# A decoder layer's feed-forward block: Strassen's seven products for gate and up, and the down projection in a second phase

## The chip, the cores and the metric

The kernel runs on one core of a Trainium2 chip. The metric is the device time of one execution in microseconds (us); the kernel before was timed in three runs.

## The reference

One layer of a hybrid decoder, for 1024 prompt tokens (one sequence) and 64 sample tokens (8 sequences of 8). All is float32, the model width D is 1024 and the feed-forward width FF is 2816. The change is in the last part, `back`:

```python
def back(x, f, u_out, o, p):
    nsa = o.reshape(B, T, Q_W) @ p['w_nsa_o']
    mix = (f['g_conv'] * u_out + f['g_nsa'] * nsa) @ p['w_out']
    x = x + f['g1'] * mix
    h = rms_norm(x, p['ffn_norm_g']) * (1.0 + f['sc2']) + f['sh2']
    ffn = (jax.nn.silu(h @ p['w_gate']) * (h @ p['w_up'])) @ p['w_down']
    return x + f['g2'] * ffn
```

Before it the layer computes the modulation vectors, one input projection, a convolution branch and an attention branch. None of that is touched.

## The kernel before, in words

**Numbers in two pieces.** A float32 operand is split into `hi` (the value in the type `F32R`, copied by ACT) and `lo` (the rest, one subtraction on DVE or POOL). A product of 128 rows is three matmuls on TensorE (PE), hi·hi, hi·lo and lo·hi, made by `mm3` (lines 338 to 340). For the sample tokens the two pieces lie side by side in 128 columns and two matmuls do (`mm2`, lines 343 and 344). Line 152 is the copy `acopy`, line 158 is `sub_sb`, the subtraction that alternates between DVE and POOL.

**Order.** The program is written in tiles from pools with a number of buffers; a scheduler that simulates the program settles the order of each engine's queue, and the engines wait for each other by semaphores. Each engine works its queue in order.

**The stages at issue** begin near 1030 us. The *m loop* (line 1482 on) multiplies the attention output by `w_nsa_o`, merges it with the convolution branch and splits the result into `mh_` and `ml_`, in three chunks of 384, 384 and 320 tokens; in between, `w_out` is loaded and split. *The out projection* is `out_half(i, j)`: nine token tiles, two column halves, 24 matmuls of 512 columns each. Its results are scaled by the gate and added to x in the tiles `x1`, which stay in SBUF to the end. `norm2` normalizes finished tiles, transposes them on PE (line 1573), applies the modulation on DVE (line 1576, `hf`) and splits the result into the same tiles `mh_`, `ml_`, now called `h2h`, `h2l`.

**The feed-forward block.** FF is worked in NF = 22 tiles of 128. `up_tile(t)` multiplies the three chunks by the gate and the up weights (8 blocks of 128 rows each): 2 x 8 x 3 x 3 = 144 matmuls, of which 96 have 384 columns and 48 have 320. Sigmoid and two multiplications follow (lines 1659 to 1661), then the split of the activations (line 1664). After every second t, `down` multiplies the two activation tiles by `w_down`, and adds the scaled sum into `x1` (lines 1697 and 1698), eleven times 18 pieces: nine token tiles by two halves. So gate/up and down alternate in one long run of matmuls, and the activations never leave SBUF:

```python
        for t in range(NF):
            up_tile(t)
            if t % 2 == 0 and t:
                down([t - 2, t - 1], False)
        down([NF - 2, NF - 1], True)
```

## Time and profile before

| | |
|---|---|
| time, median of 3 runs | 2002.25 us (1992.97 to 2007.45) |
| profiled execution, own time | 1995.01 us |
| its span, first to last instruction | 1993.2 us |
| mean granted TensorE clock | 0.981 |
| PE / DVE / ACT / POOL busy | 1903.5 / 1332.6 / 714.7 / 742.0 us |
| first matmul of gate/up, last matmul of all | 1200.06 us, ends 1985.69 us |

The views of the trace are the page with its busy times, windows (busy time of each engine in a stretch), groups of equal instructions, and the timeline of single instructions. Matmuls overlap in the pipeline: a row's length is longer than the step from one start to the next, and it is the step that a stream of them costs.

### The profile page before, as it was taken

The numbers are of one execution on the slowest core, as the hardware profiler recorded it, in microseconds if no ns is written. First come the engines' busy times: TensorE is split into PE (matmuls) and PEld (weight loads), VectorE is DVE, ScalarE is ACT, GpSimd is POOL, SyncE is SP. The second block draws the span as 40 slices with busy tenths as digits, with TensorE's granted clock in tenths as the row PEclk, the third lists the DMA queues.
The fourth block names the chain that finished last, engine by engine and source line by source line (L and its number), as shares of the span: only waits on it lengthen the run. The fifth ranks groups of instructions, "written<-read, shape, count | busy, mean of one in ns | idle before, by whom it ended". The sixth has DMA issues, their size and how long they took to land.

```text
span 1993.2 us, 29739 instructions
## 1 busy us (share of the span) xinstructions
PE 1903.5 (95%) x11036; PEld 1710.5 (86%) x11036; DVE 1332.6 (67%) x2217; ACT 714.7 (36%) x1711; POOL 742.0 (37%) x737
## 2 busy tenths in 40 slices
...
GB/s 298 180 231 219 113 110 156 104 176 110 146 176 128 177 129 126 48 14 7 1 79 223 112 1 79 61 43 43 43 54 42 43 53 33 43 53 38 48 11 90
DMA packets 170823, 191.37 MB, mean 96 GB/s; under 512 B 13847, under 2 KB 135719, under 8 KB 170606
## 3 DMA queue, kind: packets, MB, share of 16 engines
...
## 4 chain that ended last, share of the span: by engine, by line
PE 54%; DVE 2%; DMA 1%; issue 1%; POOL 1%; ACT 0%; SPq 0%; DVEq 0%; POOLq 0%; ACTq 0%
PE pf L338 10%; PE pf L339 10%; PE pf L340 10%; PE pt L340 4%; PE pt L339 4%; PE pt L338 4%; PE pT L1396 3%; PE po L1403 2%; PE po L1404 2%; PE pS L1355 1%; PE pS L1357 1%; DMA w<-in_w_out 1%; PE pS L1360 1%; DVE x L1698 0%; PE pt L343 0%
## 5 line engine op out<-in xcount | busy, mean ns | idle before, releaser
L338 PE MATMUL pf<-mh,wh 128*128 128x384 f32 (+1 forms) x1032 | 336.7, 326 | 0.0
L340 PE MATMUL pf<-mh,wl 128*128 128x384 f32 (+1 forms) x1032 | 336.5, 326 | 0.0
L339 PE MATMUL pf<-ml,wh 128*128 128x384 f32 (+1 forms) x1032 | 336.5, 326 | 0.0
L1664 POOL TENSOR_TENSOR actl<-sg,acth 128x384 fp32r<-128x384 f32 (+1 forms) x66 | 66.4, 1006 | 488.5 <-ACT acth L152 488.5
L338 PE MATMUL pd<-hh,whi 128*128 128x384 f32 (+1 forms) x576 | 194.8, 338 | 11.0 <-DVE U L1058 8.2
L338 PEld LDWEIGHTS pf<-mh,wh 128*128 128x128 f32 x1032 | 193.7, 188 | 7.3 <-DVE sg L1661 3.0
L340 PEld LDWEIGHTS pf<-mh,wl 128*128 128x128 f32 x1032 | 193.7, 188 | 4.0
L339 PEld LDWEIGHTS pf<-ml,wh 128*128 128x128 f32 x1032 | 193.7, 188 | 3.1
L339 PE MATMUL pd<-hl,whi 128*128 128x384 f32 (+1 forms) x576 | 193.2, 335 | 0.0
L340 PE MATMUL pd<-hh,wlo 128*128 128x384 f32 (+1 forms) x576 | 191.8, 335 | 1.1 <-DVE wlo L270 1.1
L1092 DVE SCALAR_TENSOR_TENSOR y<-U,wdT,y 128x1024 f32<-128x1024 f32 x120 | 162.0, 1350 | 0.6
L1698 DVE TENSOR_TENSOR x<-x,dt 128x512 f32<-128x512 f32 x180 | 146.4, 813 | 5.4
L340 PE MATMUL pt<-wdh,actl 128*128 128x512 f32 x352 | 139.0, 395 | 0.0
L339 PE MATMUL pt<-wdl,acth 128*128 128x512 f32 x352 | 138.5, 393 | 0.0
L338 PE MATMUL pt<-wdh,acth 128*128 128x512 f32 x352 | 137.1, 389 | 0.0
L1659 ACT ACTIVATE sg<-pf 128x384 f32<-128x384 f32 (+1 forms) x66 | 30.8, 467 | 295.7 <-PE pf L340 295.7
L1660 DVE TENSOR_TENSOR sg<-sg,pf 128x384 f32<-128x384 f32 (+1 forms) x66 | 34.9, 529 | 146.0 <-ACT sg L1659 146.0
L1697 DVE TENSOR_TENSOR dt<-pt,indgp 128x512 f32<-128x512 f32 x160 | 110.7, 692 | 26.3 <-PE pt L340 11.3
L338 PEld LDWEIGHTS pd<-hh,whi 128*128 128x128 f32 x576 | 110.6, 192 | 19.3 <-DVE U L1058 8.6
L1384 POOL TENSOR_SCALAR P<-P,ast 128x640 f32<-128x640 f32 (+7 forms) x128 | 89.2, 723 | 70.1 <-DVE ast L1380 68.2
L338 PE MATMUL pz<-whi,hh 128*128 128x256 f32 (+1 forms) x320 | 97.5, 306 | 18.4 <-ACT zt L152 11.3
L152 ACT ACTIVATE whi<-wraw 128x512 fp32r<-128x512 f32 (+1 forms) x133 | 81.1, 624 | 92.1 <-PE pd L339 49.5
...
## 6 DMA issues: line engine op xcount, KB each, us to landing
...
```

The lines of the kernel that those rows point to most:

```text
L152: S.activation(out, in_, AF.Copy, scale=scale)
L338: PE.matmul(out, ah, bh, start=first, stop=False)
L339: PE.matmul(out, ah, bl, start=False, stop=False)
L340: PE.matmul(out, al, bh, start=False, stop=last)
L1092: V.scalar_tensor_tensor(op, U[:, k:k + TP], wk, op, op0=ALU.mult, op1=ALU.add)
L1384: G.tensor_scalar(P_[br][g][:, :w], P_[br][g][:, :w], st[:, 2, br, g:g + 1], 1.0, op0=ALU.mult, op1=ALU.mult)
L1396: PE.transpose(pT[:nk, g * 128:(g + 1) * 128], a, ident)
L1403: PE.matmul(po, va, ph[:nk], start=(bi == 0), stop=False)
L1404: PE.matmul(po, va, pl_[:nk], start=False, stop=(bi == len(blocks) - 1))
L1664: G.tensor_tensor(al[:, c0:c0 + n], sg_[:, :n], f(ah[:, c0:c0 + n]), op=ALU.subtract)
L1697: V.tensor_tensor(tmp, p, gx[:, cs_], op=ALU.mult)
L1698: (G if last and j == 0 else V).tensor_tensor(x1[i][:, cs_], x1[i][:, cs_], tmp, op=ALU.add)
```

## The change

Everything up to the m loop stays. Then:

- The tokens are put in two columns u: u = 0 the first 512 prompt tokens, u = 1 the other 512 and the 64 sample tokens. Each u has two halves r of 256 or 288 columns (`SEG`). The split values are in quarter tiles `qh`, `ql` by row half a and segment; `ms` holds the sample's pieces for the out projection.
- `w_out` comes in blocks of 128 rows by 512 columns. The out projection does all nine tiles of j = 0 first, then those of j = 1, with `norm2` after every two tiles. `x1` is written to memory (`x1_d`) and read again at the end.
- Gate and up are the two row blocks of one matrix, and this matrix, of 2 x 2 blocks, times the 2 x 2 blocks of h is made by seven products in place of eight. `build(u)` makes the four combined right-hand blocks of h and splits them (in tiles `tq`), once; `load_up(t)` makes four combined left-hand blocks of the weights and splits all seven (tiles `aw`, one set of 14); the products' sums are made on DVE out of PSUM. Each product is 4 x 3 = 12 matmuls, of 256 columns for u = 0 and 288 for u = 1.
- The gated activations go to memory (`act_d`), not to split tiles.
- When all 22 t are done, a second phase reads `w_down` and the activations from memory and splits them. For each half j and each u it sums over all 22 t in PSUM, so that gate and residual are applied once for each token tile and half.

```diff
+    SEG = (256, 256, 288, 288)
+    qh = [[T(mp, [128, 4, w], f"qh{a}{s}", F32R) for s, w in enumerate(SEG)] for a in range(2)]
+    ql = [[T(mp, [128, 4, w], f"ql{a}{s}", F32R) for s, w in enumerate(SEG)] for a in range(2)]
...
+            last[0] = nc.sync.dma_start(raw, I["w_out"][k * 128:k * 128 + 128, j * 512:j * 512 + 512])
...
+                for sg in range(4):
+                    lo_, hi_ = max(c0, 256 * sg), min(c0 + w, TP, 256 * sg + 256)
+                    if lo_ >= hi_:
+                        continue
+                    d, e = (slice(lo_ - 256 * sg, hi_ - 256 * sg), slice(lo_ - c0, hi_ - c0))
+                    acopy(qh[a][sg][:, r, d], tn[:, e])
+                    G.tensor_tensor(ql[a][sg][:, r, d], tn[:, e], f(qh[a][sg][:, r, d]), op=ALU.subtract)
...
+    ap_ = [mkpool(uS, "aw0")]
+    xS2 = ExitStack()
+    xp1 = mkpool(xS2, "x1")
+    cp2 = mkpool(xS2, "c2")
+    x1_d = T(dp, [9, 128, D], "x1_d")
+    act_d = [T(dp, [FF // 128, 128, 2, SEG[2 * u]], f"act_d{u}") for u in range(2)]
...
+        nc.sync.dma_start(x1_d[i][:n, j * 512:j * 512 + 512], xj[:n])
+        S.activation(T(cp2, [128, 512], "xt", bufs=3)[:n], xj[:n], AF.Square, accum_out=ssq2[:n, j, i:i + 1])
         if j == 0:
...
+        V.tensor_tensor(rs2[:n, i:i + 1], ssq2[:n, 0, i:i + 1], ssq2[:n, 1, i:i + 1], op=ALU.add)
+        rsqrt_mean(rs2[:n, i:i + 1], rs2[:n, i:i + 1], D, 1)
+        for a in range(2):
+            acopy(x1[i, a][:n], x1[i, a][:n], rs2[:n, i:i + 1])
...
+    def norm2(sg):
+        u, r = sg // 2, sg % 2
+        place(sg)
+        for k in range(8):
+            pt = T(psf, [128, 512], "pt", bufs=4)
+            for j in range(2):
+                i = 2 * sg + j
+                PE.transpose(pt[:, j * 128:j * 128 + 128], x1[i, k // 4][:, k % 4 * 128:k % 4 * 128 + 128], ident)
+            hf = full[u][2 * r + k // 4][k % 4 // 2][:, k % 2]
+            V.tensor_scalar(hf, pt[:, :256], A2[:, k, 0:1], B2[:, k, 0:1], op0=ALU.mult, op1=ALU.add)
+            if r == 0 or k > 3:
+                hi, lo = (t[k // 4][sg][:, k % 4, :256] for t in (qh, ql))
+                acopy(hi, hf)
+                sub_sb(lo, hf, f(hi))
...
+    def build(u):
+
+        views = [([t[a] for t in full[u]],
+                  [[t[:, 2 * a:2 * a + 2, :256] for t in x] for x in tb[u]]) for a in range(2)]
+        if u:
+            views.append(([xs[:, 4 * a:4 * a + 4, 32 * b:32 * b + 32] for a, b in ((0, 0), (1, 0), (0, 1), (1, 1))],
+                          [[t[:, :, 256:] for t in x] for x in tb[u]]))
+        for (b11, b21, b12, b22), dst in views:
+            V.tensor_tensor(b11, b12, b11, op=ALU.subtract)
+            V.tensor_tensor(b12, b22, b12, op=ALU.subtract)
+            V.tensor_tensor(b22, b22, b11, op=ALU.subtract)
+            V.tensor_tensor(b21, b21, b22, op=ALU.subtract)
+            for src, j in ((b22, 1), (b12, 2), (b11, 0), (b21, 3)):
+                acopy(dst[j][0], src)
+                V.tensor_tensor(dst[j][1], src, f(dst[j][0]), op=ALU.subtract)
...
+    for i in range(9):
         out_half(i, 0)
-    for tiles in ((0, 1), (2,), (3, 4), (5,), (6, 7)):
-        for i in tiles:
-            if i > 2:
-                out_half(i, 0)
+    for sg in (0, 1):
+        for i in (2 * sg, 2 * sg + 1):
             out_half(i, 1)
-        norm2(tiles)
-    for j in range(2):
-        out_half(8, j)
-    woS.close()
-
-
+        norm2(sg)
+    build(0)
+    out_half(8, 1)
+    for sg in (2, 3):
+        for i in (2 * sg, 2 * sg + 1):
+            out_half(i, 1)
+        norm2(sg)
+        if sg == 2:
+            norm2s()
...
+    def atile():
+        na[0] += 1
+        early = (na[0] - 1) % 14 < 6
+        return T(ap_[0 if early else 1], [128, 512], "aw", F32R, bufs=6 if early else 8)
...
+    def load_up(t):
+
+        A = []
+        for nm in ("w_gate", "w_up"):
+            for h in range(2):
+                raw = T(fr, [128, 512], "w", bufs=6)
+                nc.sync.dma_start(raw.rearrange("p (k c) -> p k c", k=4),
+                                  I[nm][512 * h:512 * h + 512, t * 128:t * 128 + 128].rearrange("(k p) c -> p k c", p=128))
+                A.append(raw)
+        a11, a12, a21, a22 = A
+        op = {}
+
+        def split(p, src, e):
+            hi, lo = atile(), atile()
+            acopy(hi, src)
+            e.tensor_tensor(lo, src, f(hi), op=ALU.subtract)
+            op[p] = [x.rearrange("p (k c) -> p k c", k=4) for x in (hi, lo)]
+
+
+        split(1, a11, V)
+        split(2, a12, V)
+        s1 = T(stg[0], [128, 512], "s1", bufs=2) if stg else T(fr, [128, 512], "w", bufs=6)
+        V.tensor_tensor(s1, a21, a22, op=ALU.add)
+        V.tensor_tensor(a21, a11, a21, op=ALU.subtract)
+        split(7, a21, V)
+        V.tensor_tensor(a11, s1, a11, op=ALU.subtract)
+        if len(ap_) < 2:
+            build(1)
+            xS2.close()
+            ap_.append(mkpool(uS, "aw1"))
+            stg.append(mkpool(uS, "st"))
+        split(6, a11, V)
+        V.tensor_tensor(a12, a12, a11, op=ALU.subtract)
+        split(5, s1, G)
+        split(3, a12, V)
+        split(4, a22, G)
+        return op
...
+    for t in range(NF):
+        op = load_up(t)
+        for u in range(2):
+            w = SEG[2 * u]
+
+            def product(p):
+                out = T(psf, [128, 512], "pf" if p in (1, 7, 2, 4) else "pt", bufs=4)[:, :w]
+                bh, bl = right(p, u)
+                for k in range(4):
+                    mm3(out, op[p][0][:, k], op[p][1][:, k], bh[:, k, :w], bl[:, k, :w], k == 0, k == 3)
+                return out
+
+            def add(out, a, b):
+                V.tensor_tensor(out, a, b, op=ALU.add)
+
+            c11, c12, c21, c22 = (T(stg[0], [128, 288], f"s{n}", bufs=2)[:, :w] for n in (11, 12, 21, 22))
+            g = T(stg[0], [128, 2, 288], "g", bufs=3)[:, :, :w]
+            acopy(c11, product(1))
+            add(c12, product(6), c11)
+            add(c21, product(7), c12)
+            p5 = product(5)
+            add(c22, p5, c21)
+            add(c12, p5, c12)
+            add(c11, product(2), c11)
+            S.activation(g[:, 0], c11, AF.Sigmoid)
+            V.tensor_tensor(g[:, 0], c11, g[:, 0], op=ALU.mult)
+            add(c12, product(3), c12)
+            S.activation(g[:, 1], c12, AF.Sigmoid)
+            V.tensor_tensor(g[:, 1], g[:, 1], c12, op=ALU.mult)
+            V.tensor_tensor(g[:, 1], g[:, 1], c22, op=ALU.mult)
+            add(c21, product(4), c21)
+            V.tensor_tensor(g[:, 0], g[:, 0], c21, op=ALU.mult)
+            nc.sync.dma_start(act_d[u][t], g)
...
+        def load_down(j, t):
+            raw = T(fr, [128, 512], "w", bufs=6)
+            nc.sync.dma_start(raw, I["w_down"][t * 128:t * 128 + 128, j * 512:j * 512 + 512])
+            hi, lo = wpl[t][:, :512], wpl[t][:, 512:]
+            acopy(hi, raw)
+            V.tensor_tensor(lo, raw, f(hi), op=ALU.subtract)
+            wds[t] = hi, lo
...
+        def load_act(u, t):
+            raw = T(fr, [128, 512], "w", bufs=6)
+            nc.sync.dma_start(raw.rearrange("p (a c) -> p a c", a=2), act_d[u][t][:, :, :256])
+            h = ring[count[0] % len(ring)]
+            count[0] += 1
+            hi, lo = h[:, :512], h[:, 512:]
+            acopy(hi, raw)
+            V.tensor_tensor(lo, raw, f(hi), op=ALU.subtract)
...
+        for j in range(2):
+            cs_ = slice(j * 512, j * 512 + 512)
+            for u in range(2):
+                pd_ = {4 * u + n: T(psf, [128, 512], ("pf", "pt")[u], bufs=4) for n in range(4)}
+                order = list(pd_)
+                if u:
+                    pd_[8] = T(psf, [128, 512], "pf", bufs=4)
+                    order = [8] + order
...
+                late = []
+                for t in range(NF):
+                    if u == 0:
+                        load_down(j, t)
+                    a = load_act(u, t)
+                    if t >= NF - LATE:
+                        late.append((t, a))
+                        continue
+                    for i in order:
+                        step(i, t, a)
+                for i in order:
+                    for t, a in late:
+                        step(i, t, a)
+                    n = 128 if i < 8 else 64
+                    xr = T(dn, [128, 512], "xr", bufs=4)
+                    nc.sync.dma_start(xr[:n], x1_d[i][:n, cs_])
+                    tmp = T(dn, [128, 512], "xt", bufs=3)
+                    V.tensor_tensor(tmp, pd_[i], G2[i == 8][:, cs_], op=ALU.mult)
+                    V.tensor_tensor(xr[:n], xr[:n], tmp[:n], op=ALU.add)
...
```

The left-hand set for the next t shares the queue of DVE with the sums of the products. The rows of DVE before, within one `up_tile` and the end of a `down` (x: the residual tiles; wdl, wl: lo pieces of weights; sg: gated activations; pf, pt: PSUM):

```order
L1698 TENSOR_TENSOR x_7_2777_12804<-x_7_2777_12804,dt_15577 128x512
L1697 TENSOR_TENSOR dt_15587<-pt_15580,indgp_13978 128x512
L158 TENSOR_TENSOR wdl_15965<-w_15962,wdh_15964 128x1024
L1698 TENSOR_TENSOR x_7_2777_12804<-x_7_2777_12804,dt_15587 128x512
L1661 TENSOR_TENSOR sg_15654<-sg_15654,pf_15629 128x384
L1660 TENSOR_TENSOR sg_15710<-sg_15710,pf_15660 128x384
L1661 TENSOR_TENSOR sg_15710<-sg_15710,pf_15685 128x384
L158 TENSOR_TENSOR wl_15782<-w_15779,wh_15781 128x1024
L1660 TENSOR_TENSOR sg_15766<-sg_15766,pf_15716 128x320
L1661 TENSOR_TENSOR sg_15766<-sg_15766,pf_15741 128x320
```

The rows of DVE after, while the products of u = 1 of one t run (L1743: sums of products; L1699: lo pieces aw of the next t's weights w; L1709, L1716: combined weights; L1755: first gating product):

```order
L1743 TENSOR_TENSOR s_3076_14539<-pt_14557,s_3075_14538 128x288
L1699 TENSOR_TENSOR aw_14674<-w_14649,aw_14673 128x512
L1743 TENSOR_TENSOR s_3077_14540<-pf_14571,s_3076_14539 128x288
L1699 TENSOR_TENSOR aw_14662<-w_14651,aw_14661 128x512
L1743 TENSOR_TENSOR s_3078_14541<-pt_14585,s_3077_14540 128x288
L1743 TENSOR_TENSOR s_3076_14539<-pt_14585,s_3076_14539 128x288
L1716 TENSOR_TENSOR w_14651<-w_14651,w_14649 128x512
L1743 TENSOR_TENSOR s_3075_14538<-pf_14600,s_3075_14538 128x288
L1699 TENSOR_TENSOR aw_14669<-w_14653,aw_14668 128x512
L1755 TENSOR_TENSOR g_14542<-s_3075_14538,g_14542 128x288
L1743 TENSOR_TENSOR s_3076_14539<-pt_14616,s_3076_14539 128x288
```

The additions into x (line 1698 before) are gone from this stretch, and sums of 288 columns stand between the pieces of the next left-hand set.

At the seam between out projection and gate/up, the queue of PE before holds transposes of the last pair of tiles among matmuls of the sample's out projection:

```order
L339 MATMUL pf_13528<-wol_2691_12312,mh_2682_12299 128x512
L340 MATMUL pf_13528<-woh_2690_12311,ml_2685_12302 128x512
L1573 MATMUL pt_13561<-ck_61,xn_13495 128x128
L1573 MATMUL pt_13568<-ck_61,xn_13495 128x128
L1573 MATMUL pt_13575<-ck_61,xn_13495 128x128
L1573 MATMUL pt_13582<-ck_61,xn_13495 128x128
L343 MATMUL pf_13617<-woh_2688_12309,mh_2682_12299 128x512
L344 MATMUL pf_13617<-wol_2689_12310,mh_2682_12299 128x512
```

After, the last transposes of the second norm are followed by products 6, 5 and 3 of the first t (L1624: transposes; x: residual tiles; tq, qh, ql: right-hand pieces; aw: left-hand pieces):

```order
L1624 MATMUL pt_13804<-ck_61,x_2942_13736 128x128
L1624 MATMUL pt_13810<-ck_61,x_2938_13698 128x128
L1624 MATMUL pt_13810<-ck_61,x_2942_13736 128x128
L338 MATMUL pt_13920<-tq_2870_13314,aw_13884 128x256
L339 MATMUL pt_13920<-tq_2871_13315,aw_13884 128x256
L338 MATMUL pt_13948<-tq_2868_13312,aw_13889 128x256
L339 MATMUL pt_13948<-tq_2869_13313,aw_13889 128x256
L338 MATMUL pt_13979<-qh_2685_12302,aw_13893 128x256
L339 MATMUL pt_13979<-ql_2693_12310,aw_13893 128x256
L340 MATMUL pt_13920<-tq_2870_13314,aw_13885 128x256
```

The sample's out projection has moved ahead of this place, and what follows the transposes reads tiles `aw` in a pool that is opened where the tiles x are given up.

The queue of DVE at the same place after (L1626: modulation of transposed tiles; L1652 to L1655: the four subtractions of `build(1)`; L1699: lo piece of product 6, then of product 3; L158: lo pieces of h):

```order
L1652 TENSOR_TENSOR qh_2927_13631<-qh_2946_13774,qh_2927_13631 128x512
L1626 TENSOR_SCALAR ql_2947_13775<-pt_13792,A_23_88,B_24_89 128x256
L1626 TENSOR_SCALAR ql_2947_13775<-pt_13798,A_23_88,B_24_89 128x256
L1652 TENSOR_TENSOR qh_2927_13631<-qh_2946_13774,qh_2927_13631 128x512
L1626 TENSOR_SCALAR ql_2947_13775<-pt_13804,A_23_88,B_24_89 128x256
L1626 TENSOR_SCALAR ql_2947_13775<-pt_13810,A_23_88,B_24_89 128x256
L1699 TENSOR_TENSOR aw_13885<-w_13816,aw_13884 128x512
L1653 TENSOR_TENSOR qh_2946_13774<-ql_2947_13775,qh_2946_13774 128x2x256
L158 TENSOR_TENSOR ql_2695_12312<-ql_2947_13775,qh_2687_12304 128x256
L1653 TENSOR_TENSOR qh_2946_13774<-ql_2947_13775,qh_2946_13774 128x2x256
L1699 TENSOR_TENSOR aw_13894<-w_13818,aw_13893 128x512
```

Before, no such subtractions stood between the norm and the first products.

## Rows read from the trace of the kernel before

**Rows 1.** The page, part 1: busy us, share and count by engine.

```profile
PE 1903.5 (95%) x11036; PEld 1710.5 (86%) x11036; DVE 1332.6 (67%) x2217; ACT 714.7 (36%) x1711; POOL 742.0 (37%) x737
```

**Rows 2.** Windows: length, busy us (count) by engine, PEclk, DMA share, GB/s.

```profile
25.00:50.00 25.00, 24.77 (x110) 11.23 (x109) 16.31 (x27) 15.05 (x31) 13.37 (x14) 1.00 0.94 306
1050.00:1075.00 25.00, 18.14 (x99) 16.88 (x100) 21.88 (x27) 11.37 (x19) 18.83 (x18) 0.97 0.92 276
1072.00:1077.00 5.00, 4.05 (x14) 4.05 (x15) 1.92 (x3) 0.52 (x1) 4.07 (x6) 0.66 0.47 127
1137.00:1200.00 63.00, 63.00 (x309) 52.98 (x308) 40.87 (x81) 19.63 (x44) 13.48 (x21) 1.00 0.03 9
1300.00:1985.00 685.00, 685.00 (x3748) 640.38 (x3747) 354.97 (x495) 109.94 (x169) 138.12 (x110) 1.00 0.15 45
```

**Rows 3.** Groups by shape on PE, 1200 to 1995: busy, mean ns | idle.

```profile
L338 PE MATMUL pf<-mh,wh 128*128 128x384 f32 x688 | 230.5, 335 | 0.0
```

**Rows 4.** Timeline of PE, four stretches: start, length, what, count.

```profile
225.79 0.28 PE L338 MATMUL pz<-whi,hh 128*128 128x256 f32 x1
...
231.94 0.28 PE L339 MATMUL pz<-wlo,hh 128*128 128x256 f32 x1
...
1142.13 0.60 PE L1573 MATMUL pt<-ck,xn 128*128 128x128 f32 x4
...
1149.34 0.27 PE L1573 MATMUL pt<-ck,xn 128*128 128x128 f32 x1
...
1305.69 0.33 PE L338 MATMUL pf<-mh,wh 128*128 128x384 f32 x1
...
1310.37 0.33 PE L338 MATMUL pf<-mh,wh 128*128 128x384 f32 x1
...
1312.36 0.31 PE L338 MATMUL pf<-mh,wh 128*128 128x320 f32 x1
...
1315.88 0.31 PE L338 MATMUL pf<-mh,wh 128*128 128x320 f32 x1
```

**Rows 5.** Groups by shape on DVE, 1200 to 1995.

```profile
L1697 DVE TENSOR_TENSOR dt<-pt,indgp 128x512 f32<-128x512 f32 x160 | 110.7, 692 | 26.3 <-PE pt L340 11.3
...
L1661 DVE TENSOR_TENSOR sg<-sg,pf 128x320 f32<-128x320 f32 x22 | 10.7, 488 | 22.1 <-PE pf L340 22.1
```

**Rows 6.** Line 1698: count, shortest/median/longest ns, first and last start.

```profile
L1698 DVE TENSOR_TENSOR x<-x,dt x180: 683/693/1985, 1273.5 to 1945.2; 128x512 f32<-128x512 f32 x180
L1698 POOL TENSOR_TENSOR x<-x,w x9: 1266/1289/1674, 1964.3 to 1985.9; 128x512 f32<-128x512 f32 x9
```

**Rows 7.** Groups by shape on DVE, 1087 to 1200.

```profile
L1576 DVE TENSOR_SCALAR hf<-pt,A,B 128x256 f32<-128x256 f32 x22 | 11.4, 541 | 5.3 <-PE pt L1573 3.4 <-POOL ml L158 1.4
...
L158 DVE TENSOR_TENSOR ml<-hf,mh 128x256 fp32r<-128x256 f32 x10 | 4.2, 421 | 0.2
...
L158 DVE TENSOR_TENSOR ml<-hf,mh 128x128 fp32r<-128x128 f32 x8 | 2.9, 359 | 0.2
```

**Rows 8.** Groups by shape on POOL, 1027 to 1200.

```profile
L158 POOL TENSOR_TENSOR ml<-hf,mh 128x256 fp32r<-128x256 f32 x10 | 8.9, 892 | 27.0 <-ACT mh L152 27.0
...
L253 POOL TENSOR_TENSOR rs<-rs,ck 128x1 f32<-128x1 f32 x8 | 5.0, 630 | 19.9 <-DVE rs L252 19.8
```

**Rows 9.** Groups by shape on ACT, 1027 to 1200.

```profile
L1607 ACT ACTIVATE xn<-x 128x1024 f32<-128x1024 f32 x8 | 8.5, 1059 | 14.8 <-DVE x L1598 14.7
...
L152 ACT ACTIVATE wn<-wnraw 128x512 fp32r<-128x512 f32 x6 | 3.7, 617 | 1.0 <-PE pS L340 1.0
```

**Rows 10.** Timeline of the end, PE and then DVE.

```profile
1984.62 0.39 PE L340 MATMUL pt<-wdh,actl 128*128 128x512 f32 x1
...
1985.30 0.39 PE L340 MATMUL pt<-wdh,actl 128*128 128x512 f32 x1
1986.52 1.16 DVE L1698 TENSOR_TENSOR x<-x,w 128x512 f32<-128x512 f32 x1
```

**Rows 11.** Groups by shape on PEld, 1200 to 1995.

```profile
L339 PEld LDWEIGHTS pf<-ml,wh 128*128 128x128 f32 x1032 | 193.7, 188 | 3.1
```

More of the change, by code (lines that the diff above doesn't have):

```diff
@@ L1486, in emit @@
             if m in WOM:
-                load_wo(WOM.index(m), T(cp2, [128, 8, 128], "woraw", bufs=2))
+                for k in range(2):
+                    load_wo(0, 2 * WOM.index(m) + k, T(cp2, [128, 512], "woraw", bufs=2))
             if w_:
@@ new lines, in emit, with gates @@
+    xS2 = ExitStack()
[3 more added lines that the diff above has]
+    act_d = [T(dp, [FF // 128, 128, 2, SEG[2 * u]], f"act_d{u}") for u in range(2)]
+    def gates(i, pool):
+        out = [T(pool, [128, D], ind, bufs=1) for ind in ("indgp", "indgs")]
+        for j in range(2):
+            gm = T(pool, [128, 512], "xt", bufs=3)
+            nc.sync.dma_start(gm[:19], g_d[i][:, j * 512:j * 512 + 512])
+            for ind, g_ in zip(("indgp", "indgs"), out):
+                pg_ = T(psf, [128, 512], "pt", bufs=4)
+                PE.matmul(pg_, C(ind)[:19], gm[:19], start=True, stop=True)
+                acopy(g_[:, j * 512:j * 512 + 512], pg_, 1.0 if i else 0.5)
+        return out
@@ L1552, in emit, with load_x1 @@
+    x1 = {}
+    def load_x1(i, j):
+        x1[i, j] = T(xp1, [128, 512], f"x1{j}", bufs=(9, 3)[j])
+        n = 128 if i < 8 else 64
+        src = I["x_prompt"][i * 128:(i + 1) * 128] if i < 8 else I["x_sample"]
+        nc.sync.dma_start(x1[i, j][:n], src[:, j * 512:j * 512 + 512])
+    ssq2 = T(cp2, [128, 2, 9], "ssq2")
+    rs2 = T(cp2, [128, 9], "rs2")
+    G1 = gates(0, cp2)
     for i in range(2):
-        load_x1(i)
-    for m in range(len(WOM), 8):
-        load_wo(m, T(fr, [128, 8, 128], "w", bufs=3))
+        load_x1(i, 0)
```

261 lines of the change are left out of this document (94 added, 167 removed).

## The prediction

> **What bounds the kernel now.** I began with the page: PE is busy 1903.5 of 1993.2 us [rows 1]. That is an average, so the windows came next, stage by stage [rows 2]. From 1300 to 1985 PE is busy 685.00 of 685.00 us at full clock, while DVE works 354.97 of them and DMA 15%; the last stretch before it, 1137 to 1200, is 63.00 of 63.00. In this part of the kernel only less matmul time, or time in which PE starts to wait, can move the end. The groups say which matmuls: the largest, of gate and up, has no idle time ahead of it [rows 3].
>
> What a matmul costs is its step, not its row. In the timeline 52 steps of 256 columns take 231.94 - 225.79 = 6.15 us, 0.1183 each; 27 steps of 384 take 4.68 us, 0.1733; 24 steps of 320 take 3.52 us, 0.1467 [rows 4]. The three lie on a line (0.00043 us a column and 0.0082 us fixed), which puts a step of 288 at 0.1325, an estimate between two measured widths.
>
> **Gate and up, the gain.** Before, one t has 96 x 0.1733 + 48 x 0.1467 = 23.68 us. After, seven products of 12 matmuls for each u: 84 x 0.1183 + 84 x 0.1325 = 21.07 us. The saving is 2.61 us a t, 22 x 2.61 = **57.4 us**. (Columns alone would give 1/8 of 521 us, 65 us; the fixed part of 24 more matmuls takes 7 back.) It holds only if PE still finds its operands, which costs DVE: 4 combinations and 5 lo pieces of 512 elements, 14 sums out of PSUM and 8 gating products of 256 or 288. At 0.69 for 512 elements [rows 5, 6], and 0.42 to 0.46 for 256 and 288 (between 0.421 and 0.488 [rows 5, 7]), that is 9 x 0.69 + 22 x 0.44 = 15.9 us. POOL makes two lo pieces a t, 1.29 us each by its nearest row. One row shows what POOL may do to DVE: the addition into x takes 693 ns in the median and up to 1985, longer by 1.29, one whole instruction of POOL [rows 6]. With both blocked in full it is 15.9 + 2.6 = 18.5 us, still under 21.07. The additions into x of before (two a piece, 18 pieces every second t) go, which pays for most of this.
>
> There is one set of left-hand tiles, so those of the next t can be written only as products of u = 1 let them go. In the order of DVE the pieces stand between the sums of u = 1. Following that queue from the start of u = 1, lo of product 7 is ready after 9.4 to 10.3 us and is read after 11.13 + 2 x 1.42 = 13.97; the others have more room. I cost it at nothing; the cover is 3.7 us.
>
> **The seam, the loss.** Let T be the end of the out projection's last matmul. Before, PE runs on without a gap at this place [rows 2]; what it lacks after is seen in the two orders. After T, PE has products 1, 7 and 2 of the first t (36 x 0.1183 = 4.3 us), 40 transposes (a row of four is 0.60 long, of one 0.27, so 0.11 a step [rows 4]; 4.4 us) and six matmuls of products 6, 5, 3 (0.7): 9.4 us in all before it reads lo of product 6. PE's order puts product 1, four transposes, products 7 and 2 and four more transposes ahead of the first finished block of the third pair of tiles, so DVE can begin its modulation at T + 4.9 (1.4 + 0.5 + 2.8 + a little). From there to that lo piece its queue holds 16 modulations of 0.541, four lo pieces of 0.421, eight instructions of 512 (sums, gate, sample, lo) at 0.69, seven of 128 at 0.36 and four of one column at some 0.2 [rows 5, 7]: 8.7 + 1.7 + 5.5 + 2.5 + 0.8 = 19.2; so T + 24.1. PE waits 24.1 - 9.4 = 14.7 us. The next wait is for product 6 of u = 1, whose right-hand piece comes out of `build(1)` another 9.1 us of DVE later (eleven instructions of 512, two of 256, two small ones), while PE has 6.6 us to do: 2.5. Together 17.2 us if DVE never waits itself. It does once, on the last norm tile: square on ACT (half of the 1.059 row, and its accumulator), sum, POOL's power (0.630) behind four lo pieces of 0.892, two scalings of 0.617 on ACT, then the transposes [rows 8, 9]. That round is 3.4 us with POOL free and 7 with POOL's queue full; DVE's other work covers little of it, and I take 6.5, since the four pieces do stand in POOL's queue. The seam costs **23.7 us**, with 17 and 32 (POOL blocking DVE in full: seven or eight of its instructions, 8 us) as ends. The pool of the tiles `aw` that product 6 needs is opened where `x1` ends, so that no scheduler can take this work earlier.
>
> Behind an idle time the clock falls: from 1072 to 1077, where PE had waited for 0.95 us of the five and before, the granted clock is 0.66 in the mean [rows 2], that is 3.4 us at the 1.2 GHz level in which 1.7 us of work are lost. One or two such stretches: 2.5 us.
>
> The Trainium skill, "SBUF — State Buffer", section "SBUF: two separate sides", has the lock of DVE and GpSimd as exclusive: the loser waits for the whole instruction of the other. By that rule the seam would be at its upper end, 8 us more. The row's median of 693 against a longest of 1985 agrees in kind, and shows that most instructions escape it.
>
> **The smaller terms.** m loop: more and smaller copies on ACT (5 us) and subtractions on POOL (6 us) against 6.9 us in which PE idles between 1050 and 1075 alone [rows 2], and `w_out` in rows of 2 KB in place of 512 bytes: 0, between -4 and +4. Second phase: matmuls of 512 columns as before, 0.227 a step [rows 10], and no more of them. The first half of each j needs 512 KB for each t in 12 x 0.227 = 2.7 us, 193 GB/s. The trace shows 306 and 276 GB/s in stretches with a DMA share of 0.94 and 0.92 [rows 2], and ring and pieces hold some seven t ahead. ACT then has 1.23 us and DVE 1.38 a t, under 2.7. Cost 0; the change of phase, where accumulators wait for the last products and the first loads, 0 to 2, I take 1. At the end, DVE's last 512 product and sum are 1.4 us in place of the 2.0 from the last matmul to the last sum [rows 10]: -0.6.
>
> Sum against the profiled execution: 1995.0 - 57.4 + 23.7 + 2.5 + 1 - 0.6 = **1964.2 us**. The median of the runs before stands 7.2 us above that execution, so 1971 us.
>
> **Rivals.**
> (a) The seam is hidden: the scheduler's order gives PE enough other work, so that only the gain remains: 2002.2 - 57.4 - 0.6 = 1944 us. For it: before, PE does not wait there for one microsecond. Against it: the order of PE has no other work left at this place.
> (b) Preparation bounds phase one. The piece for product 7 has 3.7 us of room; if POOL blocks DVE in full and ACT's copies come late by as much, u = 1 waits 0.5 to 1.4 us a t, 11 to 30 us, and the seam stands at its upper end: 1982 to 2010, 1992 in the middle. For it: the longest rows of DVE [rows 6]. Against it: u = 0 leaves DVE 5 us.
> (c) Slower: the second phase starves. In the halves u = 0, 44 tiles t need 0.524 MB per 2.7 us. The price is 44 x (0.524 MB / rate - 2.7 us): at 160 GB/s 25 us, at 128 GB/s 61, at 110 GB/s 91. The gain of 31 is gone below 153 GB/s; below 128 GB/s the time is over 2032. For it: this stage moves 45 GB/s today [rows 2], so nothing shows these loads at speed, and each has a copy and a subtraction behind it before its buffer comes free. Against it: 276 GB/s [rows 2].
> (d) The extra matmuls bring extra weight loads, 168 a t in place of 144. If each had to lie by itself between matmuls, a t would cost 168 x 0.188 = 31.6 us [rows 11], against 23.68 now: +174 us, 2176. But then 144 of them would need 27.1 us, and the trace has 23.68; at 256 columns the step is 0.118, shorter than the load's row.
> The Trainium skill, "TensorE: Matmul & The Clock Gate", section "The mechanism", has a load overlap running matmuls only where the row groups differ; all of these use all rows. Its rule would make (d) true; the steps of this trace speak against it.
> (e) The change does not do what it says: the order has 84 matmuls for each t and u, so this is out.
>
> **How the numbers follow.** My case, 1960 to 1982: 0.57. (a) 0.12, 1942 to 1958. (b) 0.18, mostly 1982 to 2000. (c) 0.08, half of it over 2022. (d) 0.01. A rest of 0.04 for costs of the m loop and the phase change, on the slow side. A measurement of this kernel tells 1% (20 us) from no change: faster is below 1982, slower above 2022. Faster: 0.57 + 0.12 = 0.69. Same: 0.16 from (b), 0.03 from (c) and 0.02 of the rest, 0.21. Slower: 0.05 from (c), 0.01 from (d), 0.02 each from the far end of (b) and the rest, 0.10. The range takes in (a) from 1943, my case and (b) up to 1999, and leaves out the 0.15 or so above.
>
> **What would show it.** Right: steps of 0.118 and 0.132 in gate and up with PE at 100% between t = 1 and t = 21 (21.1 us a t); a hole of 20 to 27 us in PE around 1190 to 1235, ended by DVE's lo pieces and by `build`; full rate in the second phase. Wrong: waits of PE for `aw` in every t (b), for act or w_down copies in the second phase (c), or no hole at the seam (a).

## The result, and the profile after

The changed kernel takes 1967.9 us (median of 4 runs, 1961.67 to 1970.77) beside 2001.52 of the kernel before on the same chip: ratio 0.9838, interval 0.9803 to 0.9872, 33.6 us less. In another comparison (below) it was 1962.18 beside 1997.84, ratio 0.9816 (0.9781 to 0.9851). The forecast was 1971, which is 31 us less.

The profiled execution took 1967.16 us, its span is 1965.4. Its first part, which is the same program in both kernels, ran 14 us longer than in the trace of before: the last matmul of attention's value product starts at 1046.83 in place of 1032.86, and most of the delay arises between 135 and 205 us. In the traces of the experiments, all with this same first part, that matmul starts anywhere from 1026 to 1052. (Of the twelve traces behind the one of before, eleven are later than it, so whether the first part is later on average after the change, and takes back a few us of the gain, stays open.) So stages are compared from there on:

| stage, us | before | after |
|---|---|---|
| m loop, to the first matmul of the out projection | 53.8 | 48.2 |
| out projection to the end of the last matmul | 899.0 | 865.8 |
| last matmul to the end of the span | 7.5 | 4.5 |
| sum | 960.4 | 918.5 |

The changed part is 41.8 us shorter in this pair of traces. One figure ahead of the prediction has to be set right for what follows: in the trace of before, the first matmul of gate and up starts at 1192.20, not at 1200.06. Forty of them stand among the last transposes, which is how that kernel filled its seam:

```profile
1192.20 0.34 PE L338 MATMUL pf<-mh,w 128*128 128x384 f32 x1
```

The page after, by engine (it answers to [rows 1]):

```profile
PE 1856.5 (94%) x11564; PEld 1663.7 (85%) x11564; DVE 1390.0 (71%) x2574; ACT 839.9 (43%) x2042; POOL 650.7 (33%) x656
```

Windows after: length, busy us (count) of PE, PEld, DVE, ACT, POOL, then granted clock, DMA share, GB/s. The first two are of the seam, the third of gate and up, the last of the second phase with both loads (they answer to [rows 2]):

```profile
1203.00:1208.00 5.00, 4.10 (x19) 4.10 (x20) 2.66 (x6) 1.97 (x4) 2.14 (x1) 0.50 0.18 52
1220.00:1232.00 12.00, 10.26 (x40) 7.72 (x40) 10.34 (x16) 5.39 (x13) 5.17 (x4) 0.50 0.15 44
1300.00:1690.00 390.00, 390.00 (x3109) 389.60 (x3108) 287.96 (x582) 133.43 (x258) 52.09 (x36) 1.00 0.28 88
1816.00:1889.00 73.00, 73.00 (x324) 60.42 (x323) 37.44 (x63) 25.44 (x48) 0.00 (x0) 1.00 0.63 191
```

In gate and up PE has no idle time and full clock, as before, and DVE is busy 288 of 390 us, 15.5 us a t. In the second phase PE is full too, with DMA at 191 GB/s. In the two windows of the seam the granted clock is 0.50, the lower level of 1.2 GHz.

The timeline of PE, first matmuls of u = 0 and u = 1 of one t and of the next t (answers to [rows 4]):

```profile
1267.59 0.28 PE L338 MATMUL pf<-qh,aw 128*128 128x256 f32 x1
...
1277.39 0.29 PE L338 MATMUL pf<-qh,aw 128*128 128x288 f32 x1
...
1288.59 0.28 PE L338 MATMUL pf<-qh,aw 128*128 128x256 f32 x1
```

84 matmuls of 256 columns take 9.80 us, 0.1167 each, and 84 of 288 take 11.20, 0.1333. One t is 21.00 us, and so is every later one.

What PE waited for from 1100 to the end: us in all, times, longest.

```profile
PE pt L1624 <- ACT x L152: 9.8, 3, 7.1
PE pt L1548 <- DMA xt<-g_d: 2.9, 1, 2.9
PE pf L338 <- ACT aw L152: 1.2, 1, 1.2
PE pt L340 <- DVE aw L1699: 0.8, 1, 0.8
```

Two places are left: the seam, and the gate rows (`g_d`) at the start of the second phase. The seam on PE; the bracket is the idle time ahead and what ended it:

```profile
1197.98 0.28 PE L338 MATMUL pf<-qh,aw 128*128 128x256 f32 x1
...
1201.93 0.73 PE L1624 MATMUL pt<-ck,x 128*128 128x128 f32 x4 [2.38 <-ACT x L152]
1203.90 0.58 PE L338 MATMUL pf<-tq,aw 128*128 128x256 f32 x1 [1.25 <-ACT aw L152]
...
1219.72 1.12 PE L1624 MATMUL pt<-ck,x 128*128 128x128 f32 x4 [7.09 <-ACT x L152]
...
1224.76 0.55 PE L338 MATMUL pt<-tq,aw 128*128 128x256 f32 x1 [0.45 <-DVE ql L1626]
...
1228.09 0.58 PE L340 MATMUL pt<-tq,aw 128*128 128x256 f32 x1 [0.83 <-DVE aw L1699]
```

The out projection's last matmul ends its step at 1197.98, where product 1 begins; the second t begins at 1246.59. In these 48.6 us stand 21.0 us of matmuls of one t and 4.4 of transposes at full clock. **The seam costs 23.2 us**: 12.7 us are holes, all up to 1228.09, and in the rest PE works slowly, mostly at half clock. DVE in the same stretch:

```profile
1202.50 1.28 DVE L1658 TENSOR_TENSOR tq<-aw,tq 128x512 fp32r<-128x512 f32 x2
1203.71 0.15 DVE L252 SCALAR_TENSOR_TENSOR rs<-rs,ck 128x1 f32<-128x1 f32 x1
...
1209.51 1.90 DVE L1626 TENSOR_SCALAR qh<-pt,A,B 128x256 f32<-128x256 f32 x4 [3.85 <-PE pt L1624]
...
1216.28 0.68 DVE L1585 TENSOR_TENSOR xt<-pf,indgp 128x512 f32<-128x512 f32 x1
...
1221.66 1.90 DVE L1626 TENSOR_SCALAR qh<-pt,A,B 128x256 f32<-128x256 f32 x4 [2.15 <-PE pt L1624]
...
1226.49 1.55 DVE L1699 TENSOR_TENSOR aw<-w,aw 128x512 fp32r<-128x512 f32 x1
1227.96 1.21 DVE L1653 TENSOR_TENSOR qh<-ql,qh 128x512 f32<-128x512 f32 x1
1229.10 1.50 DVE L158 TENSOR_TENSOR ql<-ql,qh 128x256 fp32r<-128x256 f32 x1
```

A chain of instructions of 512 steps by 0.60 us, though each row is 0.68 long; modulations (L1626) by 0.455. DVE is busy nearly all the time, but it waits 3.9 us ahead of 1209.51 and 2.2 ahead of 1221.66, both times for transposes, while the gate product of tile 7 (L1585 at 1216.28), whose matmuls had ended at 1198, stands in its queue behind the third norm's work. POOL there:

```profile
1203.93 2.14 POOL L253 TENSOR_TENSOR rs<-rs,ck 128x1 f32<-128x1 f32 x1 [2.82 <-DVE rs L252]
...
1219.33 0.58 POOL L253 TENSOR_TENSOR rs<-rs,ck 128x1 f32<-128x1 f32 x1 [0.42 <-DVE rs L252]
...
1226.22 1.27 POOL L1699 TENSOR_TENSOR aw<-w,aw 128x512 fp32r<-128x512 f32 x1
...
1228.59 1.73 POOL L1699 TENSOR_TENSOR aw<-w,aw 128x512 fp32r<-128x512 f32 x1
```

The power (L253) takes 2.14 us beside a busy DVE and 0.58 beside an idle one. Beside POOL's subtractions (rows L1699, and one of L158 between them), DVE's instructions at 1226.49, 1227.96 and 1229.10 take 1.55, 1.21 and 1.50 in place of 0.68, 0.68 and 0.41.

The start of the second phase on PE:

```profile
1699.62 0.39 PE L340 MATMUL pf<-tq,ql 128*128 128x512 f32 x1
1702.89 5.99 PE L1548 MATMUL pt<-xt,ck 19*128 19x512 f32 x8 [2.88 <-DMA xt<-g_d]
...
1709.40 0.63 PE L339 MATMUL pf<-tq,ql 128*128 128x512 f32 x1
1709.83 0.63 PE L340 MATMUL pf<-tq,ql 128*128 128x512 f32 x1
```

PE waits 2.9 us for the gate rows; the eight records of the gate matmuls then take 5.99 us, against 3.6 ahead of the out projection, and the next product matmuls step by 0.43, half clock.

The end, PE and then DVE (answers to [rows 10]):

```profile
1960.43 0.39 PE L340 MATMUL pt<-qh,tq 128*128 128x512 f32 x1
1961.58 0.69 DVE L1838 TENSOR_TENSOR xr<-xr,xt 128x512 f32<-128x512 f32 x1
```

### The profile page after: what moved, and what is told of

Read it like the earlier page. It is cut to its first block, busy times and chain, and to the rows that moved or that the text cites. A ratio compares the mean times of both kernels' runs of the same rounds, so it can differ in the third digit from the quotient of the medians.

```text
span 1965.4 us, 32301 instructions
## 1 busy us (share of the span) xinstructions
PE 1856.5 (94%) x11564; PEld 1663.7 (85%) x11564; DVE 1390.0 (71%) x2574; ACT 839.9 (43%) x2042; POOL 650.7 (33%) x656
## 4 chain that ended last, share of the span: by engine, by line
PE 51%; DVE 3%; DMA 2%; issue 1%; ACT 1%; POOL 1%; SPq 0%; DVEq 0%; ACTq 0%; POOLq 0%
PE pf L338 7%; PE pf L339 7%; PE pf L340 7%; PE pt L340 5%; PE pt L338 5%; PE pt L339 5%; PE pT L1396 3%; PE po L1403 2%; PE po L1404 2%; PE pS L1355 1%; PE pS L1357 1%; DMA w<-in_w_down 1%; PE pf L344 1%; PE pf L343 1%; PE pS L1360 1%
## 5 line engine op out<-in xcount | busy, mean ns | idle before, releaser
L1699 POOL TENSOR_TENSOR aw<-s,aw 128x512 fp32r<-128x512 f32 x21 | 28.2, 1344 | 308.0 <-ACT aw L152 308.0
L152 ACT ACTIVATE aw<-w 128x512 fp32r<-128x512 f32 x133 | 83.3, 628 | 89.5 <-PE pf L339 60.8
L338 PE MATMUL pz<-whi,hh 128*128 128x256 f32 (+1 forms) x320 | 97.9, 307 | 18.4 <-ACT zt L152 15.5
L340 PEld LDWEIGHTS pd<-hh,wlo 128*128 128x128 f32 x576 | 110.1, 191 | 3.5 <-DVE wlo L270 1.7
L339 PEld LDWEIGHTS pd<-hl,whi 128*128 128x128 f32 x576 | 110.2, 191 | 2.6 <-issue 0.5
L1400 DVE TENSOR_TENSOR pl<-pT,ph 128x512 fp32r<-128x512 f32 (+1 forms) x148 | 99.1, 680 | 18.0 <-ACT ph L152 16.7
L338 PE MATMUL pf<-tq,aw 128*128 128x256 f32 (+1 forms) x352 | 102.0, 290 | 1.2 <-ACT aw L152 1.2
L338 PE MATMUL pt<-tq,aw 128*128 128x256 f32 (+1 forms) x352 | 102.3, 291 | 0.6 <-DVE ql L1626 0.5
L340 PE MATMUL pt<-tq,aw 128*128 128x256 f32 (+1 forms) x352 | 102.0, 291 | 0.8 <-DVE aw L1699 0.8
L339 PE MATMUL pt<-tq,aw 128*128 128x256 f32 (+1 forms) x352 | 102.3, 291 | 0.0
L339 PE MATMUL pf<-tq,aw 128*128 128x256 f32 (+1 forms) x352 | 101.9, 290 | 0.0
L954 POOL TENSOR_TENSOR vv<-kraw,vv 128x256 fp32r<-128x256 f32 x80 | 82.7, 1059 | 57.8 <-ACT vv L152 57.6
L339 PE MATMUL pf<-ql,aw 128*128 128x256 f32 (+1 forms) x352 | 101.8, 289 | 0.0
L338 PE MATMUL pf<-qh,aw 128*128 128x256 f32 (+1 forms) x352 | 101.7, 289 | 0.0
L340 PE MATMUL pf<-qh,aw 128*128 128x256 f32 (+1 forms) x352 | 101.7, 289 | 0.0
```

The costliest lines, as they stand in the source:

```text
L152: S.activation(out, in_, AF.Copy, scale=scale)
L338: PE.matmul(out, ah, bh, start=first, stop=False)
L339: PE.matmul(out, ah, bl, start=False, stop=False)
L340: PE.matmul(out, al, bh, start=False, stop=last)
L954: G.tensor_tensor(vv[:, :, 1], r, f(vv[:, :, 0]), op=ALU.subtract)
L1400: V.tensor_tensor(pl_[:nk], pT[:nk], f(ph[:nk]), op=ALU.subtract)
```

## The experiments

"Seam" is the time from the end of the out projection to the start of the third t, less one t; in some kernels matmuls of the first two t are mixed, so that the second t has no clean start. The common part is left out of the stage columns and is in the times.

| kernel | time, us | ratio to before | m loop | seam | one t | second phase |
|---|---|---|---|---|---|---|
| changed | 1967.9 | 0.9838 (0.9803 to 0.9872) | 48.2 | 48.6 | 21.0 | 273.4 |
| changed_again | 1962.2 | 0.9816 (0.9781 to 0.9851) | 49.8 | 49.1 | 21.0 | 273.7 |
| eight | 2014.2 | 1.0078 (1.0042 to 1.0114) | 47.1 | 39.5 | 24.0 | 270.4 |
| gates_mid | 1957.1 | 0.9769 (0.9713 to 0.9825) | 47.9 | 48.7 | 21.0 | 267.1 |
| warm | 1960.5 | 0.9790 (0.9729 to 0.9851) | 48.3 | 47.6 | 21.0 | 273.2 |
| rows512 | 1976.4 | 0.9878 (0.9820 to 0.9936) | 56.3 | 48.1 | 21.0 | 270.8 |
| tiles_first | 1960.4 | 0.9772 (0.9716 to 0.9829) | 48.5 | 40.2 | 21.0 | 271.1 |
| p6_ms | 1962.3 | 0.9796 (0.9746 to 0.9847) | 48.2 | 46.9 | 21.0 | 272.7 |
| hf_act | 1959.6 | 0.9794 (0.9747 to 0.9842) | 48.9 | 51.6 | 21.0 | 271.7 |
| no_pool | 1962.5 | 0.9795 (0.9746 to 0.9844) | 47.3 | 46.8 | 21.0 | 270.5 |
| cover | 1966.4 | 0.9843 (0.9796 to 0.9890) | 50.8 | 55.5 | 21.0 | 276.5 |
| best | 1950.4 | 0.9760 (0.9724 to 0.9797) | 48.4 | 39.5 | 21.0 | 265.5 |

The times scatter by the chance of the common part, so that differences of a few us are read from the stages, where one trace stands for each kernel; the out projection itself varied from 103.0 to 106.2 us there, by one stretch at half clock or none. Where an edit leaves a stage as it is, the m loop took 47.1 to 50.8 us, the seam 48.1 to 49.1 and the second phase 270.4 to 273.7 (276.5 in cover); a smaller difference is not read.

**eight.** Eight plain products in the new frame.

```diff
...
-                for k in range(4):
-                    mm3(out, op[p][0][:, k], op[p][1][:, k], bh[:, k, :w], bl[:, k, :w], k == 0, k == 3)
+                for a in range(2):
+                    bh, bl = qh[a][2 * u + r], ql[a][2 * u + r]
+                    for k in range(4):
+                        mm3(out, op[2 * row + a + 1][0][:, k], op[2 * row + a + 1][1][:, k], bh[:, k, :w], bl[:, k, :w],
+                            a == k == 0, a == 1 and k == 3)
...
```

> The frame of the changed kernel with eight plain products in place of seven (no combined blocks, no sums on DVE; the result is the same function). Theory, the seven products pay and the new frame costs: gate and up take 96 x (0.1166 + 0.1334) = 24.0 us a t in place of 21.0, +66 us, and the seam between out projection and gate/up shrinks by 10 to 18 us since nothing is combined there: 2010 to 2028 us, above the kernel before. Rival, it is the second phase with its sums in PSUM that pays: the time stays under that of the kernel before, below 1995 us.

It is 0.4 to 1.1% slower than the kernel before. Its timeline of PE, first matmul of a t and of the next:

```profile
1303.18 0.28 PE L338 MATMUL pf<-qh,aw 128*128 128x256 f32 x1
...
1327.18 0.28 PE L338 MATMUL pf<-qh,aw 128*128 128x256 f32 x1
```

24.0 us a t, 3.0 more, 66 in all; its seam is 39.5 with 24.0 + 4.4 of work, a loss of 11.1 in place of 23.2. So the whole gain is in the seven products, and about half of the seam belongs to their preparation.

**gates_mid.** The gate matmuls of the second phase moved into its first accumulation.

```diff
-        G2 = gates(1, dn)
+        G2 = []
...
+                if not G2:
+                    G2 += gates(1, dn)
                 for i in order:
```

> The four gate matmuls of the second phase are emitted late in its first accumulation in place of ahead of it. Theory, PE's wait of 2.9 us for the gate rows and the half clock behind it are a cost of their own: 4 to 7 us less than the changed kernel, no gap of PE near 1700. Rival, the first loads or copies of the second phase are just as late: the gap stays under another name, 0 to 1 us less.

The second phase falls from 273.4 to 267.1 us, and PE has no gap in it. Its window, columns as above:

```profile
1687.00:1956.00 269.00, 267.80 (x1160) 217.81 (x1158) 109.04 (x205) 81.72 (x166) 0.00 (x0) 0.99 0.50 147
```

Beside the changed trace, the wait and the half clock behind it cost 6.3 us. In the other traces with this phase unchanged that wait is 1.7 to 3.2 us long (4.2 in cover), so the cost lies between 3 and 7 us.

**warm.** Eight idle matmuls in the seam's largest hole.

```diff
+        if sg == 3:
+            wz = T(psf, [128, 512], "pt", bufs=4)
+            for _ in range(8):
+                PE.matmul(wz, ident, full[1][1][1], start=True, stop=True)
```

> Eight extra matmuls of 512 columns, whose result nobody uses, run in the hole of 7.1 us ahead of the last transposes at the seam. Theory, a good part of the seam's 23 us is the clock that falls during the holes: the granted clock behind the hole is up, the first 28 products of 256 columns step near 0.118 and not 0.213, and the time falls by 2 to 6 us. Rival, only the wait itself costs: no gain, or up to 4 us more where the extra matmuls outlast the hole.

The clock does stay up, as its windows after the hole show:

```profile
1212.00:1216.00 4.00, 2.88 (x16) 1.52 (x14) 3.88 (x9) 2.33 (x6) 0.94 (x2) 1.00 0.00 0
1216.00:1220.00 4.00, 3.12 (x24) 2.71 (x24) 4.00 (x5) 1.89 (x5) 3.09 (x3) 1.00 0.25 71
```

But the seam is 47.6 in place of 48.6. The timeline of its PE has the extra matmuls (L1623), the last transposes, and then waits:

```profile
1204.16 7.13 PE L1623 MATMUL pt<-ql,ck 128*128 128x512 f32 x16 [0.99 <-DVE ql L1630]
...
1212.72 1.79 PE L1628 MATMUL pt<-ck,x 128*128 128x128 f32 x8 [0.31 <-DVE qh L1630]
1214.62 0.36 PE L338 MATMUL pt<-tq,aw 128*128 128x256 f32 x1
...
1215.76 0.38 PE L338 MATMUL pt<-tq,aw 128*128 128x256 f32 x1 [0.67 <-ACT aw L152]
...
1217.00 0.38 PE L338 MATMUL pt<-qh,aw 128*128 128x256 f32 x1 [0.73 <-ACT aw L152]
...
1218.39 0.80 PE L340 MATMUL pt<-tq,aw 128*128 128x256 f32 x2
```

PE now runs the same products at full clock and waits between them for `aw` and, at 1218.39, inside a group. The half clock had lain inside waits for other engines. The first theory, that the clock costs a good part of the seam, falls: the clock costs about one us, or about two if one adds that the extra matmuls hold the last transposes up by some 0.8 us (they start 1.58 us behind ACT's scaling in place of 0.77), with half a us of scatter between traces.

**rows512.** `w_out` in rows of 512 bytes again.

```diff
-            last[0] = nc.sync.dma_start(raw, I["w_out"][k * 128:k * 128 + 128, j * 512:j * 512 + 512])
+            for q in range(4):
+                last[0] = nc.sync.dma_start(raw[:, q * 128:q * 128 + 128], I["w_out"][k * 128:k * 128 + 128, j * 512 + q * 128:j * 512 + q * 128 + 128])
```

> w_out is loaded in pieces of 128 columns, so in rows of 512 bytes as before, all else as changed. Theory, the m loop is 5.7 us shorter after the change because rows of 2 KB free the transfer queues: 3 to 6 us of that come back. Rival, it is shorter because POOL's subtractions of 1024 elements no longer hold DVE up: within 1 us of the changed kernel.

The m loop is 56.3 us in place of 47 to 51. Waits in it, the first two of rows512, the last two of the changed kernel at the same place:

```profile
DVE tq L1494 <- ACT tq L152: 7.0, 5, 2.2
DVE tn L1513 <- DMA tn<-th_d: 5.2, 5, 1.8
```

```profile
DVE tn L1512 <- DMA tn<-th_d: 4.3, 5, 1.5
DVE tq L1493 <- ACT tq L152: 1.2, 1, 1.2
```

The time of the stage went the way of the theory, by 8 us in place of 3 to 6. But the run shows neither that the size of the rows is the reason nor that the rival is out. It issues four times as many loads, the pieces of a block 0.48 us apart in one queue with the others, and the scheduler puts ACT's and DVE's work in another order; the kernel before had rows of 512 bytes too, but eight blocks in one load. The transfers themselves hardly differ: the queue of the loads moved 10.65 MB in 63.0% of the 56.3 us here, 10.86 MB in 73.0% of 48.2 us in the changed kernel and 10.23 MB in 63.7% of 53.8 us before, so 0.30, 0.31 and 0.30 MB for each busy us. By these numbers the rows alone are worth about 1 us (an estimate). Why the m loop became shorter stays open.

**tiles_first.** The last four tiles of the out projection ahead of the third norm.

```diff
...
-    for sg in (2, 3):
-        for i in (2 * sg, 2 * sg + 1):
-            out_half(i, 1)
-        norm2(sg)
-        if sg == 2:
-            norm2s()
+    out_half(4, 1)
+    out_half(5, 1)
+    norm2s()
+    out_half(6, 1)
+    out_half(7, 1)
+    norm2(2)
+    norm2(3)
```

> The last four token tiles of the out projection are all emitted ahead of the second norm of the third pair, so that their gate, sum and square no longer stand in DVE's queue behind that norm's modulations. (The pool of x has one more tile, that of temporaries one less.) Theory, the seam is one queue of DVE with two waits of DVE in it, 3.9 and 2.2 us: both shrink, the hole of 7.1 us goes, and the stretch from the end of the out projection to the second t falls from 48.6 to 42 to 46 us. Rival, the last norm's round over ACT and POOL sets the end whatever the order: 48 us or more.

The seam is 40.2 us, 8.4 less and under the forecast's 42; one to four us of that have moved ahead, into an out projection of 107.4 us (103.0 to 106.2 in the others), so that 4 to 7 us remain. Its waits of PE and its window of the seam, 37.9 of 40.1 us of DVE busy:

```profile
PE pt L1624 <- ACT x L152: 4.7, 3, 2.6
```

```profile
1204.57:1244.66 40.09, 31.79 (x199) 28.12 (x197) 37.92 (x79) 22.12 (x49) 13.18 (x11) 0.87 0.15 47
```

**p6_ms, hf_act, no_pool.** Three ways to take work off the seam: product 6 made early in a free tile; the 16 modulations on ACT; no subtraction on POOL.

```diff
+                hi, lo = flat(ms)[:, :512], flat(ms)[:, 512:]
...
+                S.activation(hf, pt[:, :256], AF.Identity, bias=B2[:, k, 0:1], scale=A2[:, k, 0:1])
...
-        split(5, s1, G)
+        split(5, s1, V)
...
-        split(4, a22, G)
+        split(4, a22, V)
```

> The left-hand pieces of product 6 of the first t lie in the tile ms, which is free by then, and are made ahead of build(1), so that they wait for no residual tile. Theory, DVE's queue sets the seam and PE's matmuls only stand in its gaps: product 6 moves into a hole and takes its own 12 matmuls out of what follows, 0 to 1.5 us off the 48.6 us from the out projection's end to the second t. Rival, the release of the residual tiles is what the seam waits for: 4 us or more off.

> The 16 modulations of the last two pairs of tiles are done on ACT in place of DVE. Theory, DVE's queue sets the seam: 16 x 0.455 = 7.3 us leave it, and the stretch from the end of the out projection to the second t falls by 4 to 7 us from 48.6. Rival, the chain over ACT, POOL and PE sets it and ACT becomes the queue: less than 1.5 us off, or more time.

> The lo pieces of products 5 and 4 are made on DVE in place of POOL, 1.2 us more of DVE in each t (15.5 to 16.7 of 21.0), and nothing of POOL beside it. Theory, PE sets the pace of gate and up with some 4 us of cover: 21.0 us a t as before, total within 3 us of the changed kernel. Rival, the preparation of the left-hand set is close to the bound: 21.2 us a t or more, 5 us or more in all.

p6_ms gains 1.7 us, a little over its forecast and little more than its own 12 matmuls (1.4): the release of the residual tiles isn't what the seam waits for. no_pool keeps 21.0 us a t and gains 1.8 us at the seam, where two of POOL's subtractions no longer stand beside DVE's. hf_act went against the theory: DVE is rid of 7.3 us and the seam is 3.0 us longer. Its last transposes wait longer than before, and on ACT the squares of tiles 6 and 7 (L1593) come behind copies and modulations:

```profile
1204.79 1.11 PE L1624 MATMUL pt<-ck,x 128*128 128x128 f32 x4 [8.50 <-ACT x L152]
1197.67 1.05 ACT L152 ACTIVATE qh<-ql 128x256 fp32r<-128x256 f32 x3
1198.78 0.63 ACT L1593 ACTIVATE xt<-x 128x512 f32<-128x512 f32 x1
...
1202.38 0.63 ACT L1593 ACTIVATE xt<-x 128x512 f32<-128x512 f32 x1 [1.76 <-DVE x L1586]
```

So DVE's load alone doesn't set the seam. It is a chain over ACT, DVE, POOL and PE, in which the queue that is longest at the turn of the last tiles decides.

**cover.** Six extra additions of 512 on DVE in each t.

```diff
+        if t:
+            dm = T(stg[0], [128, 512], "dm", bufs=1)
+            for _ in range(6):
+                V.tensor_tensor(dm, a11, a12, op=ALU.add)
```

> Six extra additions of 512 elements on DVE in each t from the second on, whose result nobody uses: DVE has about 19.1 of 21.0 us. Theory, PE sets the pace and the cover is some 4 us a t: 21.0 us a t, or up to 0.4 more where an operand comes late. Rival, the left-hand set is made on a path close to the bound: 22 us a t or more, 20 us in all.

```profile
1300.00:1510.00 210.00, 210.00 (x1682) 210.00 (x1682) 184.79 (x373) 67.06 (x131) 28.80 (x20) 1.00 0.26 79
```

DVE is busy 184.8 of 210 us, 18.5 us a t, and PE has no idle time. The seam grew by 6.9 us, since the extra work of the second t falls there.

**changed_again and best.** The changed kernel without an edit, and gates_mid, tiles_first and no_pool together.

> The changed kernel once more, without an edit, for a second trace of it. If the 14 us by which its common part was late are chance (the gathered loads near 150 to 200 us), this trace has another lateness there and the same 48 us m loop, 48.6 us seam and 21.0 us a t; if the change caused it, the lateness is again 10 us or more.

> Three edits of the runs before together: gates of the second phase inside its first accumulation, the last four tiles of the out projection ahead of the second norm, and all lo pieces of the left-hand set on DVE. Theory, they act at different places and add up: the stretch from the out projection's end to the second t about 38 to 41 us, the second phase about 267 us, 8 to 15 us less than the changed kernel in all, 1953 to 1960 us. Rival, they share a wait and the sum is half of that.

changed_again: the common part ended at 1039.8 us, 7 late in place of 14, beside stages within 2 us of the first trace, so that the lateness varies, but lies between the two cases of the expectation. best has 907.3 us behind the common part, against 918.5 and 922.7 of the changed kernel, so 11 to 15 less, and 1950.4 us with a ratio of 0.9760 (0.9724 to 0.9797). The time is a little under the 1953 to 1960 of the forecast. The single gains, 3 to 7, 4 to 7 and about 2, sum to 9 to 16: the three edits add up.

## Why the prediction was right

It was right in sign, size and place, in part by luck: in the stages the gain is 38 to 42 us (960.4 less 922.7 and 918.5), more than the forecast's 31, and only the times, with their chance of the common part, come as close as 34 and 36. Step by step, with what was forecast, what the trace shows, and how far that is tested:

- **Gate and up, -57.4: measured 22 x (23.68 - 21.00) = -59.0.** Both steps came out within 0.002 us of the forecast. (Its aside is loose: 24 more matmuls at 0.0082 take 4 of those 7 us back; the rest is the fixed part of the 144 that stay.) That the seven products are the gain was tested by eight (24.0 us a t, and slower than before). The cover on DVE was tested by cover and no_pool; 15.9 us of DVE a t were forecast, 15.5 measured.
- **The seam, 23.7 and 2.5 for the clock: 23.2 in all.** The sum is about right, its terms are not. Modulations began at T + 11.5, not T + 4.9, because the third pair's norm stood behind `build(0)` in DVE's queue and behind a power of 2.14 us on POOL. The piece of product 6 was ready at T + 30, not T + 24.1, although instructions of 512 step by 0.60 and not 0.69. Against the 9.4 us of work that is 20.7 us lost up to there, where the forecast had 14.7 and 6.5: of the round of the last tile that it put on top DVE waited 2.2 us, while the late start of the third norm cost 6.6; that the sum is alike is luck. The sign was a hole of 20 to 27 us; the trace has 12.7 us in eight holes, the longest 7.1, since PE worked at half clock in between. Waiting and slow working are one loss here: warm shows that the half clock by itself costs about one to two us, so that the forecast's 2.5 on top of the wait is at the upper end of what that run leaves.
- **The order, not only the load, sets the seam.** The forecast had DVE's queue as the one that decides, and one round of the last tile over ACT and POOL on top. tiles_first shows the order to be as large: with the same work in another order the seam lost 8.4 us, 4 to 7 of them net. hf_act shows that DVE's load alone isn't it.
- **m loop, 0 between -4 and +4: -5.7** (-4.0 in the second trace). The rows of 2 KB were named and weighed against the smaller copies as equal. The stage became shorter; which of its changes did that, rows512 doesn't tell. This is the term most off beside the next one.
- **Change of phase, 1 between 0 and 2: 6.3** (3 to 7 over the traces). The wait of the gate matmuls for their rows wasn't seen: their load stands in a pool that opens only when gate and up are done. gates_mid takes it back entirely.
- **End, -0.6: -3.0.** The last sum ends 1.4 us after the last matmul in place of 2.0; the span then ends 3.1 us after it in place of 5.5.
- **Rivals.** (b), preparation as the bound, is out by cover; (c), the starved second phase, by its window with 191 GB/s and no gap; (d) by steps of 0.117 with 168 weight loads a t; (a), a hidden seam, by the trace. The lock between DVE and POOL that the Trainium skill, "SBUF — State Buffer", section "SBUF: two separate sides", describes is seen at the seam, in both directions (rows of POOL and DVE above). In these rows DVE's three long instructions are 2.5 us over their usual length and POOL's power is 1.6 over, so the lock's price there is about 4 us (an estimate) and not 8. no_pool, which takes two of POOL's instructions away and gives their work to DVE, gains 1.8 us.

These terms sum to -59.0 + 23.2 - 5.7 + 6.3 - 3.0 = -38.2, beside 41.8 between the two traces. Counted by the steps of all matmuls the rest is found: gate and up 523.4 us before and 462.0 after, so -61.4; the out projection with all its transposes 107.4 in both; down with its gates 268.2 and 273.2, so +5.0, the change of phase included; with the seam, the m loop and the end that is -41.9. Why gate and up took 2.4 us more before than 22 x 23.68 wasn't tested. The forecast's sum of -31 is 11 short of that: 4 in gate and up, 3 in the seam with its clock and 2 at the end, while the gain of the m loop and the loss in the second phase, both unforeseen, cancel but for 2. That the times came closer than that is the chance of the first part.
